# Small pads shift the split weights and the transposed activations to 96 bytes modulo 128

## The chip, the cores and the metric

The kernel runs on one core of a Trainium2 chip. The metric is the device time of one execution in microseconds: 2710.3 us before, the median of three runs between 2710.04 and 2711.56.

## The reference, cut to what matters

Two stacks of transformer blocks run one after the other on 256 tokens of width 1024, in float32. Nearly all of the arithmetic is large matrix products with weights that are used once.

```python
def conv_ffn(h, w_up, conv_w, conv_b, w_down):            # first stack, 2 blocks
    u = causal_dwconv(h @ w_up, conv_w, conv_b)
    g, val = jnp.split(u, 2, axis=-1)
    return (jax.nn.gelu(g) * val) @ w_down

def swiglu(x, w13, w2):                                   # second stack, twice in each of 4 blocks
    gate, up = jnp.split(x @ w13, 2, axis=-1)
    return (jax.nn.silu(gate) * up) @ w2
...
x = first_block(...)      # mixers: RG-LRU, gated linear attention
return second_block(...)  # mixers: sparse attention, forgetting attention, latent attention, sparse attention
```

## The kernel before

**Split products.** A float32 operand is split into a high part (`hi`, rounded to the type float32r) and a low part (`lo`, the rest). A product of two split operands is three TensorE matmuls: high by high, and the two mixed ones. `mm_b` (lines 432 to 434) keeps a block of transposed activations (128 by 128) in the array, as the stationary operand, and streams a weight piece of up to 512 columns past it, as the moving operand. `mm_a` (lines 439 to 441) does it the other way round: a 128 by 128 block of weights is stationary, and the 256 tokens of the transposed activations are moving. In a row of the trace the moving operand stands first: `u<-hThi,hi` streams `hThi` past stationary weights `hi`, `y<-hi,hT` streams weights `hi` past stationary activations `hT`.

**Weights.** One DMA on SyncE's queue brings a group of pieces, at most 1024 columns, into one of 4 buffers `raw`. ScalarE copies it into `hi` (line 369) and VectorE subtracts to give `lo` (line 370); both have 9 buffers in the kernel's long-lived pool `P`.

**Stages.** `Block1.run` opens a pool for each stage of the first stack; `Block2.run` keeps one pool `Q` for the second. In a feed-forward of the second stack the first two chunks of 256 hidden columns go through `mm_b` for each half of the tokens (the leads, stationary `hThi` and `hTlo`); the other nine go through `mm_a` in `ffn_both`; and the way down goes through `mm_b` with the hidden activations `hT` as stationary operand, 24 products after a chunk and 48 for each half of the tokens at the end. In the first stack the convolutional feed-forward does the same with `dhi` and `dlo`. Output projections use `oThi` and `oTlo` (second stack), `xchi` and `xclo` or `oT` (first stack) as stationary operand.

**What sets the order.** The order of the instructions is that of the Python code, with a scheduler that sees operations and buffers. A tile's address comes from its pool alone: tiles are laid one behind the other in the order in which they are first asked for, each rounded up to 32 bytes per partition. Every matmul operand here starts at a multiple of 128 bytes from its tile's start, except for pieces whose width isn't a multiple of 32 columns: the 272-column pieces of the forgetting attention (`mx1.v0`) and the 16-column blocks of `gla.z`.

Of the kernel before, what the change touches and what calls it, by code (L numbers as in the profile page):

```python
# [8 lines left out]
F32 = mybir.dt.float32  # L9
# [244 lines left out]
class _Cols:  # L254
    def __init__(self):
        self.at, self.parts, self.n = {}, [], 0
# [72 lines left out]
class Weights:  # L329
# [33 lines left out]
    def _load(self, g):  # L363
        nc = self.nc
        r, w = self._raw(g), self.groups[g][1]
        hi, lo = (self.pool.tile([128, w], F32R, name=f"{p}{g}", tag=p, bufs=self.nsp) for p in ("hi", "lo"))
        for a in range(0, w, self.step):
            b = min(a + self.step, w)
            nc.scalar.copy(out=hi[:, a:b], in_=r[:, a:b])  # L369
            nc.vector.tensor_tensor(out=lo[:, a:b], in0=r[:, a:b], in1=hi[:, a:b].bitcast(F32), op=OP.subtract)  # L370
        self.split[g] = (hi, lo)
# [5 lines left out]
class Kernel:  # L377
    def __init__(self, tc, a, out, plan, at, stages1, stages2):
        self.tc, self.nc, self.a, self.out, self.at = tc, tc.nc, a, out, at
        self.stages1, self.stages2 = stages1, stages2  # L380
        with ExitStack() as es:
            self.P = es.enter_context(tc.tile_pool(name="p", bufs=1))
            self.ps = es.enter_context(tc.tile_pool(name="ps", bufs=1, space=PSUM))
            self.ws = Weights(tc, self.P, a["w"], plan, 4, 9)
            self.idx = [0, 0]
            self.ident = self.P.tile([128, 128], F32, name="ident")
            make_identity(self.nc, self.ident)
            self.expo = self.P.tile([128, 4], F32, name="expo")
            self.nc.gpsimd.memset(self.expo, -0.5)
            self.first = {}  # L390

            self.hT = [self.P.tile([128, 8, 256], F32R, name=f"hT{p}") for p in ("hi", "lo")]
            self.x = [self.P.tile([128, D], F32, name=f"x{t}") for t in range(2)]
            for t in range(2):
                self.nc.sync.dma_start(out=self.x[t], in_=a["x"][t * 128:t * 128 + 128])
            if stages1:
                with tc.tile_pool(name="b1", bufs=1) as self.Q:
                    Block1(self).run()
            if stages2:
                self.ws.step = 512  # L400
                with tc.tile_pool(name="b2", bufs=1) as self.Q:
                    Block2(self).run()
            else:
                for t in range(2):
                    self.nc.sync.dma_start(out=out[0, t * 128:t * 128 + 128, :], in_=self.x[t])

    def small(self, name, w=1):
        return self.P.tile([128, w], F32, name=name, tag=f"sm_{name}_{w}", bufs=2)
# [59 lines left out]
class Block1:  # L468
# [534 lines left out]
    def run(self):  # L1003
        k = self.k
        self.ones = self.Q.tile([128, 128], F32, name="ones")
        self.V.memset(self.ones, 1.0)
        self.ada_init()
        end = x = None
        for st in k.stages1:
            i = {"rg": 0, "gla": 1}.get(st[0], st[-1])  # L1010
            w = int(st[0] == "cf")
            last = st == k.stages1[-1]
            if x is None and st[0] != "rg":
                x = self.h_tiles()
                mods = self.pre_mods(i, w)
                self.pre(0, mods, x)
                end = [1, mods, x]
            with k.tc.tile_pool(name=f"st_{st[0]}{i}", bufs=1) as self.R:
                stage = self.rg() if st[0] == "rg" else self.gla(x) if st[0] == "gla" else self.conv_ffn(i, x)
                if st[0] != "rg":  # L1020

                    next(stage)
                    self.pre(*end) if len(end) == 3 else self.turn(*end)
                self.due = self.left = DUE[i, w]
                self.share = 0.0
                y = next(stage)
                row = self.gate_row(i, w)
                h = None
                if not last:
                    mods = self.pre_mods(i + w, 1 - w)  # L1030
                    h = self.h_tiles()
                end = [0, y, row, mods if h else None, h]
                self.turn(*end)
                end[:2] = 1, next(stage)
                for _ in stage:
                    pass
                x = h
        if k.stages2:
            k.xt(0)
        self.turn(*end)  # L1040
        k.idx[1] = k.idx[0]


class Block2:
    def __init__(self, k):
        self.k, self.nc, self.a, self.P, self.Q = k, k.nc, k.a, k.P, k.Q
        self.V, self.ACT = k.nc.vector, k.nc.scalar
        self.gbt, self.shared, self.v, self.vt = {}, {}, [None, None], {}

    def gb(self, i):  # L1050
# [51 lines left out]

    def ht(self, key, c):

        if (key, c) not in self.hT:
            self.hT[key, c] = self.Q.tile([128, 2, 2, 256], F32R, name="hT", tag="kT", bufs=4)
        return self.hT[key, c]
# [93 lines left out]
    def attend(self, t, g, qh, kh, v, mask, scale, oT):  # L1201


        k, Q, V, ACT, nc = self.k, self.Q, self.V, self.ACT, self.nc
        nk = 128 * (t + 1)
        sm = k.small("sm", 4)

        sp = [k.bank("u", 4, (128, 2, 256)) for _ in range(2)]
        scores = [sp[e % 2][:, e // 2, :nk] for e in range(4)]
        for e in range(4):  # L1210
            nc.tensor.matmul(scores[e], qh(e), kh(e), start=True, stop=True)  # L1211
        probs = []
        for e in range(4):
            s = Q.tile([128, 256], F32, name="s", tag="s1k", bufs=5)[:, :nk]
            nb = k.small(f"nb{e}")
            V.tensor_tensor_reduce(out=s, in0=scores[e], in1=mask[:, :nk], scale=-scale, scalar=3.0e38,
                                   op0=OP.add, op1=OP.min, accum_out=nb)
            ACT.activation(out=s, in_=s, func=AF.Exp, scale=-1.0, bias=nb, accum_out=sm[:, e:e + 1])
            probs.append(s)
        rc = k.small("rc", 4)  # L1220
        V.reciprocal(out=rc, in_=sm)
        for e in range(4):
            V.tensor_scalar(out=probs[e], in0=probs[e], scalar1=rc[:, e:e + 1], scalar2=None, op0=OP.mult)
        pTs = []
        for e0 in (0, 2):
            pt = k.bank("u", 4, (128, 2, 2, 128))
            pT = Q.tile([128, 2, 2, 128], F32, name="pT", tag="pT", bufs=2)
            for e in range(2):
                for j in range(t + 1):
                    nc.tensor.transpose(pt[:, e, j, :], probs[e0 + e][:, j * 128:j * 128 + 128], k.ident)  # L1230
            (ACT.copy if e0 else V.tensor_copy)(out=pT[:, :, :t + 1, :], in_=pt[:, :, :t + 1, :])
            pTs.append(pT)

        op = k.bank("u", 4, (128, 2, 128))
        for e0 in (0, 2):
            for j in range(t + 1):
                for e in range(2):
                    nc.tensor.matmul(op[e * 64:e * 64 + 64, e0 // 2, :], v[j][:, e0 + e, :], pTs[e0 // 2][:, e, j, :],  # L1238
                                     start=j == 0, stop=j == t)
        if not oT:  # L1240
            oT += [Q.tile([128, 8, 128], F32R, name=f"oT{p}", tag=f"oT{p}{t}", bufs=1) for p in ("hi", "lo")]
        k.split(oT[0][:, g * 2:g * 2 + 2, :], oT[1][:, g * 2:g * 2 + 2, :], op)

# [312 lines left out]
```

## Time and profile before

| | |
|---|---|
| median of the runs | 2710.3 us |
| the profiled execution's own time | 2707.17 us |
| its span, first to last instruction | 2705.4 us |
| TensorE busy | 2643.8 us, 98% |
| VectorE busy | 1922.6 us, 71% |
| ScalarE busy | 1413.3 us, 52% |
| GpSimd busy | 76.6 us, 3% |
| weight loads into the array | 2335.4 us, 86%, beside the matmuls |
| read from HBM | 510.44 MB, 189 GB/s over the span |
| granted TensorE clock, mean | 0.996 of full speed |

A matmul's recorded duration runs from its start to its modelled end and overlaps the next ones, so durations of a line add up to more than the span. What a product costs in a stream is the step from its start to the start of the next. The stretches below run from the start of the first of N products to the start of the last, so that N-1 steps lie in them. The x in such a row counts what is busy in the stretch, and so also a product that began just before it.

### The profile page before, as it was taken

What the parts mean: (1) busy time and instruction counts of PE and PEld (TensorE: products, weight loads), DVE (VectorE), ACT (ScalarE), POOL (GpSimd) and SP (SyncE); (2) the same over time, 40 slices, a digit from 0 to 9 for tenths busy, and PEclk for the clock granted to TensorE, in tenths of its full rate; (3) what the DMA queues carried; (4) which work ended last, traced back from release to release, by engine and by line L of the source; (5) the groups of instructions that cost most, each with busy time, mean ns of one, the idle gap of its engine ahead of it and who ended that gap; (6) DMA issues with size and microseconds to landing.
All of it is one profiled execution on the core that took longest, in us unless ns stands there. A gap on an engine that the chain in (4) does not pass through costs nothing.

```text
span 2705.4 us, 44260 instructions
## 1 busy us (share of the span) xinstructions
PE 2643.8 (98%) x16680; PEld 2335.4 (86%) x16680; DVE 1922.6 (71%) x3876; ACT 1413.3 (52%) x2848; POOL 76.6 (3%) x115
## 2 busy tenths in 40 slices
PE   7899989999999999999999999999999999999998
PEld 5689977899899779989987899899889989977898
DVE  6889889877666886575666855756885575687755
ACT  4665664655444655444455544544754454456542
POOL 0000000000000000000000000000000000000000
PEclk9999999999999999999999999999999999999999
DMA  8868774665655547656654565664455565453652
GB/s 312 295 228 305 226 246 168 223 201 164 212 185 164 165 126 219 185 182 200 185 174 125 187 184 169 214 183 149 155 171 187 172 207 184 156 182 122 212 186 94
DMA packets 141081, 514.39 MB, mean 190 GB/s; under 512 B 16177, under 2 KB 16561, under 8 KB 139330
## 3 DMA queue, kind: packets, MB, share of 16 engines
q1 hardware_dynamic: 140866, 511.56, 58.9%
q8 instruction: 131, 2.15, 0.3%
q14 instruction: 84, 0.69, 0.1%
HBM read 510.44 MB, written 1.05 MB: 189 GB/s over the span
## 4 chain that ended last, share of the span: by engine, by line
PE 84%; issue 6%; DVE 5%; DMA 2%; ACT 2%; POOL 1%; DVEq 0%; POOLq 0%; SPq 0%; ACTq 0%
PE u L439 13%; PE u L440 13%; PE u L441 13%; PE y L432 11%; PE y L434 11%; PE y L433 11%; PE u L432 2%; PE u L433 2%; PE u L434 2%; DVE lo L370 2%; PE u L1211 1%; PE u L1238 1%; PE u L1230 1%; PE u L463 1%; DMA raw<-w 1%
## 5 line engine op out<-in xcount | busy, mean ns | idle before, releaser
L370 DVE TENSOR_TENSOR lo<-raw,hi 128x512 fp32r<-128x512 f32 (+4 forms) x1501 | 1080.7, 746 | 539.1 <-ACT hi L369 528.1
L369 ACT CAST hi<-raw 128x512 fp32r<-128x512 f32 (+4 forms) x1501 | 951.5, 666 | 772.0 <-issue 448.0
L439 PE MATMUL u<-hThi,hi 128*128 128x256 f32 x3016 | 857.4, 284 | 2.5 <-ACT hi L369 1.4
L440 PE MATMUL u<-hTlo,hi 128*128 128x256 f32 x3016 | 855.2, 284 | 0.0
L441 PE MATMUL u<-hThi,lo 128*128 128x256 f32 x3016 | 854.8, 284 | 0.2 <-DVE lo L370 0.2
L439 PEld LDWEIGHTS u<-hThi,hi 128*128 128x128 f32 x3016 | 578.8, 192 | 7.1 <-ACT hi L369 1.6
L440 PEld LDWEIGHTS u<-hTlo,hi 128*128 128x128 f32 x3016 | 579.1, 192 | 4.6 <-issue 1.0
L441 PEld LDWEIGHTS u<-hThi,lo 128*128 128x128 f32 x3016 | 578.8, 192 | 0.5 <-DVE lo L370 0.4
L432 PE MATMUL y<-hi,hT 128*128 128x512 f32 x704 | 279.1, 396 | 0.0
L433 PE MATMUL y<-lo,hT 128*128 128x512 f32 x704 | 278.6, 396 | 0.0
L434 PE MATMUL y<-hi,hT 128*128 128x512 f32 x704 | 278.4, 395 | 0.0
L432 PE MATMUL y<-hi,hThi 128*128 128x512 f32 (+6 forms) x504 | 189.3, 377 | 3.5 <-ACT hThi L444 3.3
L433 PE MATMUL y<-lo,hThi 128*128 128x512 f32 (+6 forms) x504 | 185.5, 369 | 0.1
L434 PE MATMUL y<-hi,hTlo 128*128 128x512 f32 (+6 forms) x504 | 184.1, 369 | 0.2 <-DVE hTlo L445 0.2
L434 PEld LDWEIGHTS y<-hi,hT 128*128 128x128 f32 x704 | 132.4, 188 | 31.9
L432 PEld LDWEIGHTS y<-hi,hT 128*128 128x128 f32 x704 | 132.6, 188 | 29.0
L433 PEld LDWEIGHTS y<-lo,hT 128*128 128x128 f32 x704 | 132.3, 188 | 28.8
L432 PE MATMUL u<-hi,hThi 128*128 128x512 f32 x320 | 127.0, 399 | 4.8 <-ACT hThi L444 4.8
L444 ACT CAST hT<-th 128x256 fp32r<-128x256 f32 x144 | 58.3, 405 | 130.2 <-DVE th L1100 130.2
L433 PE MATMUL u<-lo,hThi 128*128 128x512 f32 x320 | 125.8, 394 | 0.0
L434 PE MATMUL u<-hi,hTlo 128*128 128x512 f32 x320 | 124.2, 394 | 0.0
L432 PEld LDWEIGHTS y<-hi,hThi 128*128 128x128 f32 x504 | 94.9, 188 | 21.1 <-ACT hThi L444 5.2
(301 smaller groups left out, 3119.3 us busy)
## 6 DMA issues: line engine op xcount, KB each, us to landing
raw<-w SPq DMA_DIRECT2D x823, 512.0 KB, 3.7
adar<-ada SPq DMA_DIRECT2D x80, 512.0 KB, 4.8
gb<-lngb SPq DMA_DIRECT2D x12, 1024.0 KB, 5.2
adag<-ada SPq DMA_DIRECT2D x8, 512.0 KB, 5.4
adag<-adag SPq DMA_DIRECT2D x8, 512.0 KB, 5.7
raw<-w SPq DMA_DIRECT2D x8, 384.0 KB, 3.0
raw<-w SPq DMA_DIRECT2D x5, 480.0 KB, 3.5
raw<-w SPq DMA_DIRECT2D x4, 396.0 KB, 3.1
```

What stands on the lines that cost most here:

```text
L369: nc.scalar.copy(out=hi[:, a:b], in_=r[:, a:b])
L370: nc.vector.tensor_tensor(out=lo[:, a:b], in0=r[:, a:b], in1=hi[:, a:b].bitcast(F32), op=OP.subtract)
L432: mm(out, xhi, w[0], start=start, stop=False)
L433: mm(out, xhi, w[1], start=False, stop=False)
L434: mm(out, xlo, w[0], start=False, stop=stop)
L439: mm(out, whi, xhi, start=start, stop=False)
L440: mm(out, whi, xlo, start=False, stop=False)
L441: mm(out, wlo, xhi, start=False, stop=stop)
L444: self.nc.scalar.copy(out=hi, in_=src)
L463: self.nc.tensor.transpose(p[:, k * 128:k * 128 + 128], x[:, (h + k) * 128:(h + k + 1) * 128], self.ident)
L1211: nc.tensor.matmul(scores[e], qh(e), kh(e), start=True, stop=True)
L1230: nc.tensor.transpose(pt[:, e, j, :], probs[e0 + e][:, j * 128:j * 128 + 128], k.ident)
```

## The change

Four kinds of tile that nothing reads or writes are asked for at the right moments, so that the tiles behind them move up: 64 bytes per partition in front of `hi` and `lo`, 96 at the head of every stage's pool in the first stack, 96 in front of `hT`, 64 in front of `oThi` and `oTlo`.

```diff
     def _load(self, g):
         nc = self.nc
         r, w = self._raw(g), self.groups[g][1]
+        if not self.split:
+            self.pool.tile([128, 16], F32, name="padw")
         hi, lo = (self.pool.tile([128, w], F32R, name=f"{p}{g}", tag=p, bufs=self.nsp) for p in ("hi", "lo"))
...
+    def pad(self, pool, name, n):
+
+        pool.tile([128, n], F32, name=f"pad{name}")
...
             with k.tc.tile_pool(name=f"st_{st[0]}{i}", bufs=1) as self.R:
+                k.pad(self.R, st[0], 24)
...
     def ht(self, key, c):
 
+        if not self.hT:
+            self.k.pad(self.Q, "h", 24)
         if (key, c) not in self.hT:
...
         if not oT:
+            if not self.padded:
+                k.pad(Q, "o", 16)
+                self.padded = True
             oT += [Q.tile([128, 8, 128], F32R, name=f"oT{p}", tag=f"oT{p}{t}", bufs=1) for p in ("hi", "lo")]
```

The built programs of both kernels hold the same instructions in the same order on every engine, with the same waits, and differ in addresses alone. These are the addresses of the split operands, modulo 128 bytes:

| tile | role in a product | before | after |
|---|---|---|---|
| `hi`, `lo` | stationary in `mm_a`, moving in `mm_b` | 32 | 96 |
| `hThi`, `hTlo` | moving in `mm_a`, stationary in the leads and projections | 32 | 32 |
| `hT` | stationary on the way down, second stack | 64 | 96 |
| `dhi`, `dlo` | stationary on the way down, first stack | 64 | 96 |
| `xchi`, `xclo`, `oT` | stationary in output projections, first stack | 64 | 96 |
| `oThi`, `oTlo` | stationary in output projections, second stack | 0 | 96 |

`raw`, `x0` and `x1` stay at 32. The pads also move tiles that only VectorE, ScalarE and unsplit products use, for instance the working tiles `F`, `cv0` and `v0` from 64 to 96, `th` and `s` from 64 to 0, `adar` from 0 to 64.

## Rows read from the trace of the kernel before

**Rows 1.** The page: span, TensorE's busy time, granted clock by slice, chain by line.

```profile
span 2705.4 us, 44260 instructions
...
PE 2643.8 (98%) x16680; PEld 2335.4 (86%) x16680; DVE 1922.6 (71%) x3876; ACT 1413.3 (52%) x2848; POOL 76.6 (3%) x115
...
PEclk9999999999999999999999999999999999999999
...
PE u L439 13%; PE u L440 13%; PE u L441 13%; PE y L432 11%; PE y L434 11%; PE y L433 11%; PE u L432 2%; PE u L433 2%; PE u L434 2%; DVE lo L370 2%; PE u L1211 1%; PE u L1238 1%; PE u L1230 1%; PE u L463 1%; DMA raw<-w 1%
```

**Rows 2.** Groups by form: line, operands, shapes, count | busy us, mean ns | idle before.

```profile
L439 PE MATMUL u<-hThi,hi 128*128 128x256 f32 x3008 | 855.2, 284 | 2.5 <-ACT hi L369 1.4 <-DVE mn L910 1.1
...
L433 PE MATMUL y<-lo,hT 128*128 128x512 f32 x704 | 278.6, 396 | 0.0
...
L433 PE MATMUL y<-lo,hThi 128*128 128x512 f32 x352 | 139.5, 396 | 0.1
...
L433 PE MATMUL u<-lo,hThi 128*128 128x512 f32 x320 | 125.8, 394 | 0.0
...
L433 PE MATMUL y<-lo,dhi 128*128 128x512 f32 x176 | 69.8, 397 | 0.0
...
L433 PE MATMUL y<-lo,oThi 128*128 128x512 f32 x128 | 51.9, 405 | 0.0
...
L433 PE MATMUL y<-lo,oT 128*128 128x512 f32 x32 | 13.0, 406 | 0.0
...
L433 PE MATMUL y<-lo,xchi 128*128 128x512 f32 x32 | 12.9, 402 | 1.4 <-DVE lo L370 1.4
```

**Rows 3.** Six stretches: us, TensorE busy (x), granted clock, DMA share, GB/s.

```profile
144.22:154.89 10.67, 10.67 (x48) 1.00 0.72 245
841.75:863.90 22.15, 22.15 (x97) 1.00 0.36 106
1003.08:1010.13 7.05, 7.05 (x33) 1.00 0.58 181
...
1324.50:1358.93 34.43, 34.43 (x289) 1.00 0.59 171
1958.10:1960.66 2.56, 2.56 (x13) 1.00 0.00 0
318.38:327.94 9.56, 9.56 (x43) 1.00 0.59 196
```

**Rows 4.** TensorE in order of time, 272-column pieces: start us, us, line, operands.

```profile
1393.68 0.29 PE L432 MATMUL y<-hi,hThi 128*128 128x272 f32 x1
...
1394.06 0.29 PE L432 MATMUL y<-hi,hThi 128*128 128x272 f32 x1
...
1394.44 0.28 PE L432 MATMUL y<-hi,hThi 128*128 128x272 f32 x1
```

**Rows 5.** The same view, the 16-column blocks of gla.z.

```profile
369.75 0.28 PE L439 MATMUL u<-hThi,hi 128*16 128x256 f32 x1
...
370.10 0.28 PE L439 MATMUL u<-hThi,hi 128*16 128x256 f32 x1
...
370.45 0.28 PE L439 MATMUL u<-hThi,hi 128*16 128x256 f32 x1
```

**Rows 6.** Groups by form on VectorE and ScalarE: element work at different addresses.

```profile
L370 DVE TENSOR_TENSOR lo<-raw,hi 128x512 fp32r<-128x512 f32 x1291 | 849.8, 686 | 501.0 <-ACT hi L369 490.6
...
L938 DVE TENSOR_TENSOR F<-F,qT 128x512 f32<-128x512 f32 x8 | 5.5, 688 | 0.0
...
L369 ACT CAST hi<-raw 128x512 fp32r<-128x512 f32 x1291 | 752.2, 618 | 659.7 <-issue 448.0 <-PE y L434 94.9 <-DMA raw<-w 44.0
```

More of the change, by code (lines that the diff above doesn't have):

```diff
@@ L1047, in __init__ @@
         self.V, self.ACT = k.nc.vector, k.nc.scalar
+        self.padded = False
         self.gbt, self.shared, self.v, self.vt = {}, {}, [None, None], {}
```

## The prediction

> **What bounds the kernel now.** I read the page first. TensorE is busy for 98% of a span of 2705.4 us, the granted clock is full in every slice, and the chain that ended last is nearly all matmuls: `mm_a` has 39% of it, the lines of `mm_b` another 39% [rows 1]. VectorE (71%) and ScalarE (52%) mostly wait for each other's halves of a weight split. So time is the number of products times the step between two of them, and only a change of that step can pay.
>
> Then I looked for steps by operand address. The groups by form give the counts and who is stationary [rows 2]. Their mean durations run to a modelled end and hide most of the difference, so I took stretches in which one kind of product runs without a break and divided by the steps in them [rows 3]. All have a granted clock of 1.00, the 2.4 GHz level:
>
> - stationary `hThi` at 32, 512 columns: 48 products from 144.22, 10.67 us / 47 = 227.0 ns; 32 products from 1003.08 in the second stack, 7.05 / 31 = 227.4 ns
> - stationary `hT` at 64, 512 columns: 96 products from 841.75, 22.15 / 95 = 233.2 ns
> - stationary `dhi` at 64: 42 products from 318.38, 9.56 / 41 = 233.2 ns
> - stationary `oThi` at 0: 12 products from 1958.10, 2.56 / 11 = 232.7 ns
> - `mm_a`, stationary weights at 32, 256 columns: 288 products from 1324.50, 34.43 / 287 = 120.0 ns
>
> In all of them the moving operand lies at 32. So the step is not columns alone. From 256 to 512 columns with the stationary at 32 it grows by 227.4 - 120.0 = 107.4 ns; what is left of either, 12.6 ns, doesn't depend on the length. With the stationary at 64 or 0 that remainder is 18.4 ns. The address of the stationary block is the one thing that sorts the stretches: `hT`, `dhi` and `oThi` come from different stages, are written by different code, and agree to 0.5 ns, while the leads of the first and the second stack agree to 0.4 ns on the other level.
>
> **The change part by part.** No instruction, wait or queue position changes, so there is nothing to add but addresses.
>
> Way down and output projections, `mm_b` with the stationary going from 64 or 0 to 96. From the counts [rows 2], each for three lines: `hT` 704, `dhi` 176, `oThi` 128, `oT` 32, `xchi` 32, so 1072 x 3 = 3216 products of 512 columns. No stretch shows a full stationary block at 96. It lies 64 bytes from the good place, 32, and 32 bytes from each of the bad ones; and since 0 and 64, also 64 bytes apart, cost the same to 0.5 ns, I take it that the pattern repeats after 64 bytes and 96 costs what 32 costs. The gain is then 233.2 - 227.4 = 5.8 ns each: the second stack has most of these products, so its own stretches are the nearest rows. 3216 x 5.8 = 18.7 us. The ends are 2 ns, by which the recorded means of `y<-lo,hT` and `u<-lo,hThi` differ (396 and 394 ns), hence 6.4 us, and 233.2 - 227.0 = 6.2 ns, hence 19.9 us. All of it is on the path, since TensorE is what the end waits for.
>
> `mm_a`, stationary weights from 32 to 96, moving `hThi` still at 32: 3 x 3008 = 9024 products [rows 2]. By the same repeat after 64 bytes this costs nothing. The only rows with a stationary block at 96 are the 16-column blocks of `gla.z`, which lie 64 bytes apart: three products from 369.75 (at 96) take 0.35 us, three from 370.10 (at 32) take 0.35 us [rows 5]. That bounds the difference at 3 ns either way for an eighth of the columns, so it does not decide. Full blocks could move by as much as 0 and 64 differ from 32, 5.8 ns, either way: 52.3 us. I take 0 and keep both ends as rivals.
>
> Moving weights from 32 to 96 in every `mm_b`: the 272-column pieces lie at 32, 96, 32 in turn, past `hThi` at 32. Three products from 1393.68 (at 96) take 0.38 us, three from 1394.06 (at 32) take 0.38 us [rows 4]. I take 0; the resolution leaves 3 ns for each.
>
> Element work on moved tiles: the subtraction of 512 columns with all operands at 32 takes 686 ns, a multiplication of as many with all operands at 64 takes 688 ns [rows 6]. Two nanoseconds on 1291 splits are 2.6 us of an engine that idles a quarter of the span, so they cost nothing; were that cover gone, they would cost 2.6 us. TensorE running 0.7% faster asks the same of the splits: in the densest stretch, `mm_a` from 1324.50, the DMA share is 0.59 [rows 3], and ScalarE's copy idled 660 us in all, of which 44 us waited for a landing [rows 6]. I see nothing that comes late next.
>
> **Sum.** 18.7 us off. Against the profiled execution's own 2707.2 us (span 2705.4 and 1.8 around it) that gives 2688.5. The median of the runs lies 3.1 us above that execution, so the forecast is 2710.3 - 18.7 = 2691.6, say 2692.
>
> **The rivals.**
>
> *96 is a bad place for a stationary block.* The rows have one good residue, 32, and it might be the only one. Then `hT`, `dhi` and the rest go from one bad place to another, and `mm_a` leaves the good one: 9024 x 5.8 = 52 us more, 2763 us. A penalty of 18.7 us / 9024 = 2.1 ns on `mm_a` already eats the whole gain, since it has nearly three times as many products. A variant of it: 32 is good because the moving operand lies there too. Then the way down (96 and 96) gains its 19 us, `mm_a` (96 past 32) loses 52, and the total is still about 33 us slower or more. For it: nothing here shows 96 at work on a full block. Against it: 0 and 64 agree, and three products with the moving operand 64 bytes from the stationary one run as fast as with both in one place [rows 4].
>
> *96 is better than 32.* 12.6 ns of a step of `mm_a` do not come from columns, so there is something to win; if 96 took off another 5.8 ns there, as 32 does against 64, `mm_a` would bring 52 us on top: 2710.3 - 18.7 - 52.3 = 2639. No row speaks for it but the size of the remainder; the `gla.z` blocks at 96 show no gain.
>
> *Addresses don't matter.* The 5.8 ns could belong to the role, not to the address: `hThi` is always the input of a stage, the others are always its output. Then nothing moves: 2710. Against it stands that three tiles of two stacks, written by different code and read among different neighbours, share the slow level, at 0 and at 64, while the one tile at 32 has the fast level in both stacks. The Trainium skill speaks for this rival: "TensorE: Matmul & The Clock Gate", in "Step-by-step: what each phase is for", says that TensorE has two independent read ports into SBUF, one for the streaming operand and one for weight loads, so that loading the next block takes nothing from the running product. By that rule all 512-column steps would be equal and the sum would be 0; the stretches at 227.4 and 233.2 ns [rows 3] disagree with it, unless their difference has another cause than an address.
>
> **How the numbers follow.** The forecast, 96 like 32: 0.50; its own range, by the ends above, is 2690 to 2704. 96 better: 0.16, 2639. Nothing moves: 0.14, 2710 give or take 2. 96 bad: 0.20, about 2743 to 2763. The range takes in the first three and leaves the last out, since it alone has the 2 in 10 that may be left: 2639 to 2712. About 0.2%, 5.4 us, is what a measurement of this kernel can tell from no change; faster is the first two, 0.66; same 0.14; slower 0.20.
>
> **What would show it right or wrong.** In the profile after: the step of `y<-hi,hT`, over 96 products at a feed-forward's end, falls from 233.2 to about 227 ns, and so do the steps with `dhi` and `oThi`; the step of 288 products of `mm_a` stays at 120.0 ns; leads stay at 227. If `mm_a` steps at 122 ns or more, the first rival holds; at 118 or less, the second; if the way down stays at 233 and `mm_a` at 120, the third. TensorE's idle time before `mm_a` should stay at a few microseconds; were it to grow, the splits have become late and my cover for them was wrong.

## The result, and the profile after

The median goes from 2710.17 us (2707.53 to 2711.56) to 2663.8 us (2662.09 to 2668.03), four runs each: a ratio of 0.9832 with an interval of 0.9815 to 0.9849, so 46.4 us less. The forecast was 18.7 us less, 2692, with a range from 2639 to 2712. Direction and range held; the size was 2.5 times the forecast, and nearly all of it came from the product for which I had put down nothing.

In the numbering of the kernel after, `mm_b` is lines 438 to 440, `mm_a` 445 to 447, the copy into `hi` 371 and the subtraction that gives `lo` 372. First the page: span and busy time of the engines, the granted clock by slice, and the groups that answer to [rows 1, 2].

```profile
span 2662.2 us, 44260 instructions
...
PE 2598.1 (98%) x16680; PEld 2287.7 (86%) x16680; DVE 1919.3 (72%) x3876; ACT 1413.6 (53%) x2848; POOL 75.3 (3%) x115
...
PEclk9999999999999999999999999999999999999999
...
L445 PE MATMUL u<-hThi,hi 128*128 128x256 f32 x3016 | 840.1, 279 | 2.4 <-ACT hi L371 1.4
...
L445 PEld LDWEIGHTS u<-hThi,hi 128*128 128x128 f32 x3016 | 567.7, 188 | 7.1 <-DVE mn L916 1.6
```

The same instructions at the same clock: TensorE's busy time fell by 2643.8 - 2598.1 = 45.7 us, VectorE's by 3.3 us and ScalarE's not at all. One product of `mm_a` lasts 279 ns where it lasted 284.

Then the stretches, read as in [rows 3]: us, TensorE busy (x), granted clock, DMA share, GB/s. In order: 96 products of the way down with `hT`; 32 of the leads in the second stack; 96 of `mm_a` behind the first way down of a feed-forward (48 products); 96 behind the second (24 products); 288 of `mm_a`; 12 with `oThi`; 42 with `dhi` in the first stack.

```profile
835.33:857.40 22.07, 22.07 (x98) 1.00 0.36 113
996.68:1003.78 7.10, 7.10 (x33) 1.00 0.56 193
1042.54:1053.73 11.19, 11.19 (x97) 1.00 0.63 190
1059.41:1070.19 10.78, 10.78 (x96) 1.00 0.64 195
1125.28:1157.82 32.54, 32.54 (x289) 1.00 0.62 193
...
1939.67:1942.21 2.54, 2.54 (x13) 1.00 0.20 77
...
316.36:326.41 10.05, 9.80 (x43) 1.00 0.66 210
```

Divided by the steps in them:

| stretch | before | after |
|---|---|---|
| `mm_a`, 288 products | 120.0 ns | 32.54 / 287 = 113.4 ns |
| `mm_a`, 96 products behind the second way down | 120.0 | 10.78 / 95 = 113.5 |
| `mm_a`, 96 products behind the first way down | 120.0 | 11.19 / 95 = 117.8 |
| way down, `hT` | 233.2 | 22.07 / 95 = 232.3 |
| leads, `hThi` | 227.4 | 7.10 / 31 = 229.0 |
| `oThi` | 232.7 | 2.54 / 11 = 230.9 |
| first stack, `dhi` | 233.2 | 10.05 / 41 = 245.1, with 0.25 us idle in it |

So where did the 43.2 us between the two profiled executions come from (2707.2 and 2664.0)? I added the steps from the start of each product to the start of the next, by kind, over the whole of both traces: `mm_a` went from 1088.8 to 1042.2 us, -46.6; the way down with `hT` from 493.0 to 491.4, -1.6; the leads from 488.0 to 490.1, +2.1. The products with `dhi`, `xchi` and `oT` of the first stack cost 5.2 us more (127.4 to 130.4, 26.5 to 28.4, 25.8 to 26.1), everything else 1.3 us less. Together that is -42.3 us, and 0.8 us lies ahead of the first product.

The first stack kept almost nothing. Its `mm_a` won 6.6 us, but its leads took 1.3 us more, and of the 5.2 us more for `dhi`, `xchi` and `oT` the larger part is waiting for producers. Here is who TensorE waited for, in the profile after and behind it in the profile before: us in total, times, longest.

```profile
PE y L438 <- ACT dhi L450: 2.5, 4, 1.2
...
PE y L440 <- DVE dlo L451: 1.4, 5, 0.3
...
PE y L438 <- ACT hi L371: 1.2, 1, 1.2
```

```profile
PE y L432 <- ACT dhi L444: 1.3, 1, 1.3
```

Before, it waited once for the copy into `dhi`, for 1.3 us, and not at all for `dlo`; after, nine times for 3.9 us, and once more for 1.2 us ahead of a product with `xchi`. The start of the same product tells it too: the 4001st matmul, shortly behind the first stack, starts at 706.5 us after and 708.1 us before, 1.6 us earlier. The other 41.6 us came behind it.

### The profile page after: what moved, and what is told of

It reads as the page before. It is cut to its first block, busy times and chain, and to the rows that moved or that the text cites. A ratio compares the mean times of both kernels' runs of the same rounds, so it can differ in the third digit from the quotient of the medians.

```text
span 2662.2 us, 44260 instructions
## 1 busy us (share of the span) xinstructions
PE 2598.1 (98%) x16680; PEld 2287.7 (86%) x16680; DVE 1919.3 (72%) x3876; ACT 1413.6 (53%) x2848; POOL 75.3 (3%) x115
## 4 chain that ended last, share of the span: by engine, by line
PE 78%; issue 8%; DVE 7%; DMA 3%; ACT 2%; POOL 1%; DVEq 0%; SPq 0%; POOLq 0%; ACTq 0%
PE u L445 11%; PE u L446 11%; PE u L447 11%; PE y L438 10%; PE y L440 10%; PE y L439 10%; PE u L438 3%; PE u L439 3%; PE u L440 3%; DVE lo L372 2%; DMA raw<-w 2%; DMA adar<-ada 1%; PE u L1221 1%; PE u L469 1%; PE u L1248 1%
## 5 line engine op out<-in xcount | busy, mean ns | idle before, releaser
L445 PE MATMUL u<-hThi,hi 128*128 128x256 f32 x3016 | 840.1, 279 | 2.4 <-ACT hi L371 1.4
L447 PE MATMUL u<-hThi,lo 128*128 128x256 f32 x3016 | 837.0, 278 | 0.6 <-DVE lo L372 0.6
L446 PE MATMUL u<-hTlo,hi 128*128 128x256 f32 x3016 | 837.5, 278 | 0.0
L445 PEld LDWEIGHTS u<-hThi,hi 128*128 128x128 f32 x3016 | 567.7, 188 | 7.1 <-DVE mn L916 1.6
L446 PEld LDWEIGHTS u<-hTlo,hi 128*128 128x128 f32 x3016 | 567.6, 188 | 4.7 <-issue 1.0
L447 PEld LDWEIGHTS u<-hThi,lo 128*128 128x128 f32 x3016 | 569.1, 189 | 1.2 <-DVE lo L372 1.0
```

What stands on the lines that cost most here:

```text
L445: mm(out, whi, xhi, start=start, stop=False)
L446: mm(out, whi, xlo, start=False, stop=False)
L447: mm(out, wlo, xhi, start=False, stop=stop)
```

## The experiments

All kernels here compute the whole result. In the expectations, theory A (later A256) is that the step depends on the *distance*, the address of the stationary block minus that of the moving block, and no longer on either alone; theory B is my prediction's reading, that the stationary block's own place decides. Places are given modulo 128 bytes, as in the section on the change. "Distance" is always the difference modulo 256 bytes. These are the distances of the main kinds of product, from the addresses in the built programs:

| kernel | `mm_a` | leads | `hT` | `dhi`, `xchi`, `oT` | `oThi` |
|---|---|---|---|---|---|
| before | 0 | 0 | 32 | 32 | 96 |
| after | 64 | 192 | 128 | 128 | 0 |
| weights alone | 64 | 192 | 96 | 96 | 160 |
| activations alone | 0 | 0 | 64 | 64 | 192 |
| both at 96 | 0 | 0 | 64 | 32 | 224 |
| swapped | 64 | 192 | 96 | 128 | 192 |
| every distance its best | 64 | 192 | 0 | 0 | 0 |

**Halves of the change.** The first run moves the weights alone, the second the activations alone.

```diff
-                k.pad(self.R, st[0], 24)
+                k.pad(self.R, st[0], 16)
-            self.k.pad(self.Q, "h", 24)
+            self.k.pad(self.Q, "h", 16)
-                k.pad(Q, "o", 16)
+                pass
```

> Only the split weights go to 96 modulo 128; hT, dhi, xchi and oT stay at 64, oThi at 0, hThi at 32. If the gain of the change is the weights' alone, mm_a steps at 113 to 114 ns as after the change, and the time is 2710 - 9024 x 5.6 ns = 2660 plus what the 512-column products lose: about 2664. Theory A (what counts is the distance between stationary and moving block): the way down, stationary 64 past moving 96, is 32 apart as before, so it stays at 233. Theory B (what counts is the stationary block's own address): the same, 233, since it stays at 64. If instead the activations' move is needed, the time stays above 2690.

Measured: 2672.16 us, ratio 0.9854 (0.9839 to 0.9868). Rows: 96 products of the way down, 288 of `mm_a`.

```profile
836.83:859.07 22.24, 22.24 (x98) 1.00 0.33 119
1127.44:1159.99 32.55, 32.55 (x288) 1.00 0.63 194
```

```diff
-            self.pool.tile([128, 16], F32, name="padw")
+            pass
-                k.pad(self.R, st[0], 24)
+                k.pad(self.R, st[0], 8)
-            self.k.pad(self.Q, "h", 24)
+            self.k.pad(self.Q, "h", 8)
```

> Only the transposed activations hT, dhi, xchi, oT and oThi go to 96; the split weights stay at 32 with hThi at 32. mm_a stays at 120 ns. Theory A: the way down, stationary 96 past moving 32, is 64 apart like mm_a after the change, so it should gain as mm_a did, to 226 ns or less: 3216 x 6 = 19 us, about 2691. Theory B, an own address of 96 is fast: the same gain. If 96 gives the way down 232 whatever the moving block's place, the time is 2707 or so, no change.

Measured: 2711.3 us, ratio 0.9999 (0.9989 to 1.0009). The same two stretches:

```profile
844.60:866.77 22.17, 22.17 (x97) 1.00 0.34 109
1137.76:1172.18 34.42, 34.42 (x288) 1.00 0.56 184
```

The weights carry the change: with them alone at 96, `mm_a` steps in 32.55 / 287 = 113.4 ns. Without them, activations at 96 bring nothing: 22.17 / 95 = 233.4 ns, where both theories had forecast 226 or less. So 64, the distance at which `mm_a` is fast, is a slow one for 512 columns: the same rule does not hold for both lengths. Beside the moved weights the activations' move does pay: with the weights alone the time is 6 to 8 us above the kernel after, more than the expectation's 2664, and the way down then steps in 22.24 / 95 = 234.1 ns, at distance 96, against 232.3.

**Own place or distance.** The third kernel puts `hThi` and the weights both at 96, the fourth puts `hThi` at 96 and the weights at 32; the other pads keep the rest where it is needed.

```diff
+            self.pad(self.P, "t", 16)
             self.hT = [self.P.tile(
...
-            self.pool.tile([128, 16], F32, name="padw")
+            pass
```

> hThi and the split weights both at 96 (and raw, x at 96); hT at 32, dhi, xchi and oT at 0, oThi at 64. Theory A: mm_a's blocks are 0 apart as before the change, 120 ns; the leads 0 apart, 227 ns. Theory B: stationary weights at 96 are fast, mm_a at 113 to 114 ns. The way down shows stationary blocks at 32, 0 and 64 past moving 96.

Measured, one run: 2710.34 us. Rows: way down, leads, `mm_a`.

```profile
842.69:864.86 22.17, 22.17 (x97) 1.00 0.33 114
1004.06:1011.09 7.03, 7.03 (x32) 1.00 0.55 192
1135.93:1170.34 34.41, 34.41 (x288) 1.00 0.59 184
```

> The places of after are swapped: hThi at 96, the split weights at 32; hT at 0, dhi, xchi and oT at 32, oThi at 96. Theory A (distance): 64 apart again, mm_a at 113 to 114 ns. Theory B (own address of the stationary block): weights at 32 as before, 120 ns. A third, C, that the moving block's own address counts: 113 or less if 96 is a better place for the moving block, 120 if it doesn't matter.

Measured, one run: 2665.63 us; its diff is the added line above, with the weights' pad kept and two other pads changed. The same three stretches:

```profile
831.89:854.13 22.24, 22.24 (x97) 1.00 0.38 110
993.37:1000.46 7.09, 7.09 (x32) 1.00 0.60 187
1122.44:1154.99 32.55, 32.55 (x288) 1.00 0.62 192
```

These two settle it. With both operands at 96 the leads step in 7.03 / 31 = 226.8 ns and `mm_a` in 34.41 / 287 = 119.9, as with both at 32 before; the weights lie there at the same place as after the change, even modulo 256 (224), so their own place is not what makes `mm_a` fast. With weights at 32 (modulo 256 they are at 32 there and at 160 before) past `hThi` at 96, `mm_a` takes 113.4 ns, as after. `hThi` lies at 96 in both kernels, with 119.9 and with 113.4 ns, so the moving block's own place doesn't decide either. No residue is good or bad by itself; the distance sorts the steps.

**Every distance its best.** By that theory the way down should have distance 0 (its best) and `mm_a` 64. So this kernel (e9 in the expectations) keeps the weights where the change puts them and moves the activations of `mm_b` on by 128 bytes.

```diff
-                k.pad(self.R, st[0], 24)
+                k.pad(self.R, st[0], 56)
-            self.k.pad(self.Q, "h", 24)
+            self.k.pad(self.Q, "h", 56)
-                k.pad(Q, "o", 16)
+                k.pad(Q, "o", 48)
```

> Distances are now taken modulo 256 (stationary minus moving). The weights stay where the change puts them (mm_a 64 apart, 113 to 114 ns), and hT, dhi, xchi, oT and oThi go to the very residue of the weights, 0 apart modulo 256; after the change they are 128 apart (oThi 0). Theory A256: the way down steps at 228 ns like the leads before the change, 3216 products less 384 at oThi gain 4 ns each, 11 us on the time after the change: about 2652. Rival R (the way down's 232 to 234 ns belong to its role, not to any address): no gain, 2664.

Measured: 2678.59 us, ratio 0.9871 (0.9854 to 0.9888), slower than the kernel after. Rows: way down, 96 and 288 products of `mm_a`.

```profile
836.82:858.35 21.53, 21.53 (x97) 1.00 0.38 110
1060.18:1071.37 11.19, 11.19 (x97) 1.00 0.64 190
1127.16:1160.97 33.81, 33.81 (x289) 1.00 0.64 188
```

Half of it came as expected: the way down steps in 21.53 / 95 = 226.6 ns, so 128 is not the period of the pattern (after has distance 128 there, and 232.3 ns). The other half is a surprise: `mm_a` steps in 117.8 ns though its operands lie at the same places, modulo 256, as in the kernel after, which has 113.4.

**The other distances.** Four kernels like the last one, with another pad in front of the weights (the pools behind move along, so the way down stays at distance 0): 32, 96, 192 and 128 bytes between weights and `hThi`.

```diff
-            self.pool.tile([128, 16], F32, name="padw")
+            self.pool.tile([128, 8], F32, name="padw")
```

> Weights 32 bytes behind hThi modulo 256, the way down at distance 0. Theory A256: the way down at 228 ns, the leads at 224 apart, near 233 ns as oThi showed there; mm_a at a distance not yet seen: between 113 and 120 if the step rises and falls smoothly with distance. Rival R: way down at 232 to 234.

> Weights 96 bytes behind hThi modulo 256, the way down at distance 0. Theory A256: the way down at 228 ns, the leads (160 apart) near 233 ns. mm_a is new: 113 to 120; if 512-column products tell of it (234 at 96, the highest), 120 or more.

> Weights again at 96 modulo 128 as in the change, but in the other half of 256 bytes: 192 behind hThi. If 128 bytes is the period (the change's own premise), mm_a steps at 113 to 114 as after it and the time is the same. Theory A256: a distance of its own, so another step than 113.5, and the leads at 64 apart, 233.4 ns.

> mm_a at the one distance not yet seen among the multiples of 32 bytes up to 128: weights 128 behind hThi modulo 256, the way down at distance 0, the leads at 128. By the distances seen (0: 120.0, 32: 118.3, 64: 113.3 or 117.8, 96: 118.7, 192: 117.8) I expect 117 to 120 and leads at 232; if 128 has a faster step of its own, 113 or less.

Measured, one run each: 2697.13, 2699.51, 2690.58 and 2705.2 us. The stretch of 288 products of `mm_a` in the four, in that order:

```profile
1134.76:1168.72 33.96, 33.96 (x288) 1.00 0.62 187
```

```profile
1135.85:1169.91 34.06, 34.06 (x289) 1.00 0.64 187
```

```profile
1134.34:1168.14 33.80, 33.80 (x288) 1.00 0.63 188
```

```profile
1136.97:1171.40 34.43, 34.43 (x288) 1.00 0.59 184
```

That is 118.3, 118.7, 117.8 and 120.0 ns. The way down, at distance 0 in all four but each time at another place, steps in 227 ns throughout (21.55 to 21.58 us for 95 steps). All the stretches of all runs together give this picture (means of the steps between products of one kind, those over 6% above the median, which hold waits, left out):

| distance, modulo 256 | 0 | 32 | 64 | 96 | 128 | 160 | 192 | 224 |
|---|---|---|---|---|---|---|---|---|
| 512 columns (`mm_b`), ns | 228.0 | 233.1 | 233.4 | 233.9 | 232.3 | 233.4 | 229.5 | 233.1 |
| 256 columns (`mm_a`), ns | 120.0 | 118.3 | 113.3 or 117.8 | 118.7 | 120.0 | not run | 117.8, a few 113.3 | not run |

At 512 columns, 0 and 128 differ, and so do 64 and 192: the pattern doesn't repeat after 128 bytes. It does after 256: distances that agree modulo 256 but not modulo 512 have the same step (233.0 and 233.1 ns at 32, 232.3 and 232.3 at 128). The distances of `mm_a` all lay in one half of 512 bytes, so for 256 columns that period is not shown. Tiles of different stages at one distance mostly agree to 1.5 ns. The exception is `oThi`, whose products come in runs of 18 at most and mostly of 6 or fewer: at distance 0 it has 230.1 ns where `hT` has 226.7, both in the kernel with every distance at its best. Why is not shown.

**Two steps at one distance.** At distance 64 a run of `mm_a` keeps either 113.3 or 117.8 ns from its first few products to its last. After has both, as the third and the fourth of its stretches above show: of the 48 runs behind a way down in the second stack, the first of each of the 8 feed-forwards has 117.8 and the other 40 have 113.3, at the same distances. The kernel with every distance at its best has 117.8 in all 48. Is it the last product ahead of the run that chooses? Two kernels mix both distances in the way down, by a wider tile for `hT` (and, in the first, the pads in front of `hT` and `oThi` of the kernel with the best distances): the first has distance 0 for its high part and 128 for its low part, which comes last of the three products; the second has it the other way round.

```diff
-            self.hT[key, c] = self.Q.tile([128, 2, 2, 256], F32R, name="hT", tag="kT", bufs=4)
+            self.hT[key, c] = self.Q.tile([128, 2, 2, 288], F32R, name="hT", tag="kT", bufs=4)[:, :, :, :256]
```

> At 64 apart mm_a has two steps that hold through a whole run of 96 or 288 products, 113.3 and 117.8 ns: after the change it enters the first behind a way down at distance 128, in e9 the second behind a way down at distance 0. Here everything is as after the change, but the high part of hT lies at distance 0 and its low part, the stationary block of the last product ahead of mm_a, at 128. Theory L (the last product ahead decides the step that locks): mm_a at 113.3 as after the change, the way down at about (227 + 227 + 232) / 3 = 229 ns, 2112 x 3.5 = 7 us better than after the change: about 2657. Rival M (most of the products ahead decide, or the residue of the tile): 117.8, about 2682.

Measured: 2687.38 us, ratio 0.9912 (0.9896 to 0.9927). Way down and `mm_a`:

```profile
839.03:860.98 21.95, 21.95 (x97) 1.00 0.37 111
1130.42:1164.23 33.81, 33.81 (x289) 1.00 0.63 187
```

> The mirror: the high part of hT stays at distance 128 as after the change, only the low part, ahead of mm_a, goes to distance 0. Theory L: mm_a locks at 117.8, about 8 FFNs x 768 products x 4.5 ns = 28 us slower than after the change, less 2 us on the way down: about 2690. Rival M: 113.3 as after the change, 2662.

Measured, one run: 2688.3 us. The same two stretches:

```profile
834.61:856.78 22.17, 22.17 (x97) 1.00 0.35 110
1126.55:1160.35 33.80, 33.80 (x288) 1.00 0.61 187
```

Both have 117.8 ns, so the distance of the last product ahead doesn't choose; that theory falls. The rival, that most of the products ahead decide, falls with the second kernel, for which it had 113.3. The way down adds something: taken apart by line, the first kernel's three steps are 226.7, 232.6 and 234.1 ns. Only the product whose own block and whose successor's block both lie at distance 0 is fast, so one foreign distance among three spoils two steps. In the second kernel no two blocks in a row lie at distance 0, and none of the three is fast. In the mean it is 21.95 / 95 = 231.1 ns for the first and 22.17 / 95 = 233.4 for the second.

To know that the kernel after itself was stable, it ran once more beside them.

> The changed kernel itself, on the same chip as the others of this call: 2664 within 5 us; mm_a at 113.3 behind every way down.

Measured: 2666.45 us, ratio 0.9835 (0.982 to 0.9851), again with 113.3 ns in 40 of the 48 runs behind a way down. The expectation said all of them; the first of each feed-forward has 117.8, as in the first profile.

**A kick at the entry.** If the moment at which a run is entered chooses, and not the addresses, then a small shift in time should flip it. These kernels have the addresses of the one with the best distances, and split the second product of each run of `mm_a` in the second stack's feed-forwards in two (56 runs, 48 of them behind a way down): 64 and 192 columns, 128 and 128, 192 and 64.

```diff
+                            if c <= NCH - FW + 1 and not (j or s or kk):
+                                mm = self.nc.tensor.matmul
+                                mm(u[:, s, :], w[0][:, sl], x[0][:, kk, :], start=True, stop=False)
+                                mm(u[:, s, :64], w[0][:, sl], x[1][:, kk, :64], start=False, stop=False)
+                                mm(u[:, s, 64:], w[0][:, sl], x[1][:, kk, 64:], start=False, stop=False)
+                                mm(u[:, s, :], w[1][:, sl], x[0][:, kk, :], start=False, stop=False)
+                                continue
```

> The same with 64 and 192 columns, another disturbance of the entry. By the moment of entry it may lock at 113.3 (2651) where 128 does not, or the other way round; by addresses 117.8 (2679).

> All addresses as in e9; the second product of every run of mm_a behind a way down streams its 256 columns as 128 and 128. If the moment of entry chooses the step, some or all runs lock at 113.3 ns: 8 x 768 x 4.5 = 28 us off e9's 2679, 2651. If addresses choose: 117.8 and 2679 or a little more (56 extra products of some 10 ns, under 1 us).

> The same with 192 and 64 columns. The three together say whether any disturbance of the entry flips the step: by the moment of entry at least one of them steps at 113.3, by addresses none does.

Measured: 2658.91 us (0.9804, 0.9787 to 0.982), 2659.01 us (0.9804, 0.9789 to 0.9819), and 2687.99 us in one run. The entry with 64 columns in order of time (start us, us, line, operands), and then the 93 products of `mm_a` that follow the split, in the first kernel and in the third:

```profile
1040.24 0.28 PE L1159 MATMUL u<-hThi,hi 128*128 128x256 f32 x1
1040.36 0.20 PE L1160 MATMUL u<-hTlo,hi 128*128 128x64 f32 x1
1040.39 0.33 PE L1161 MATMUL u<-hTlo,hi 128*128 128x192 f32 x1
1040.56 0.30 PE L1162 MATMUL u<-hThi,lo 128*128 128x256 f32 x1
1040.70 0.28 PE L445 MATMUL u<-hThi,hi 128*128 128x256 f32 x1
```

```profile
1040.70:1051.14 10.44, 10.44 (x94) 1.00 0.65 197
```

```profile
1047.23:1058.06 10.83, 10.83 (x93) 1.00 0.63 193
```

10.44 / 92 = 113.5 ns against 10.83 / 92 = 117.7, at the same addresses. So addresses allow the short step, and what happens at the entry decides whether it is taken: two of three kicks flip all 48 runs behind a way down, the third flips none.

It is not the length of the delay, though. From the first product of the run to the first one behind the split the kernel with 64 columns takes 1040.70 - 1040.24 = 0.46 us; these are the same two products with 128 and with 192 columns first:

```profile
1041.88 0.28 PE L1159 MATMUL u<-hThi,hi 128*128 128x256 f32 x1
...
1042.34 0.28 PE L445 MATMUL u<-hThi,hi 128*128 128x256 f32 x1
```

```profile
1046.76 0.28 PE L1159 MATMUL u<-hThi,hi 128*128 128x256 f32 x1
...
1047.23 0.28 PE L445 MATMUL u<-hThi,hi 128*128 128x256 f32 x1
```

That is 0.46 and 0.47 us, so all three push what follows back by about as much, and they differ in the starts inside the entry. A plain shift in time without a split was not run.

The two kernels with a flip are faster than the kernel before by 52 us. They lie 5 to 8 us below the kernel after, but their intervals (to 0.982) and its own (from 0.9815) still touch.

At distances 0 and 64 the recorded weight loads go with the step. These are the page's groups of loads of `mm_a` before, then with the best distances and no kick, then with the kick of 64, then of 192:

```profile
L439 PEld LDWEIGHTS u<-hThi,hi 128*128 128x128 f32 x3016 | 578.8, 192 | 7.1 <-ACT hi L369 1.6
```

```profile
L447 PEld LDWEIGHTS u<-hThi,lo 128*128 128x128 f32 x3016 | 577.5, 192 | 0.6 <-DVE lo L372 0.4
L445 PEld LDWEIGHTS u<-hThi,hi 128*128 128x128 f32 x3016 | 567.1, 188 | 7.1 <-DVE mn L916 1.6
```

```profile
L445 PEld LDWEIGHTS u<-hThi,hi 128*128 128x128 f32 x2960 | 556.8, 188 | 5.5 <-ACT hi L371 2.4
L447 PEld LDWEIGHTS u<-hThi,lo 128*128 128x128 f32 x2960 | 558.5, 189 | 1.8 <-DVE lo L372 1.6
```

```profile
L445 PEld LDWEIGHTS u<-hThi,hi 128*128 128x128 f32 x2960 | 565.5, 191 | 4.2 <-ACT hi L371 1.6
L447 PEld LDWEIGHTS u<-hThi,lo 128*128 128x128 f32 x2960 | 557.8, 188 | 0.5 <-DVE lo L372 0.4
```

In a run at 117.8 ns one load of three is recorded at 192 ns and two at 188; in one at 113.3 all are at 188; before, at 120.0, all are at 192. The kick of 192 moved the long load from the third product to the first, and did not remove it. At other distances the mark fails. These are the longest loads at distance 192, where a run has 117.8 ns, and at distance 128, where it has 120.0:

```profile
L447 PEld LDWEIGHTS u<-hThi,lo 128*128 128x128 f32 x3016 | 567.4, 188 | 0.6 <-DVE lo L372 0.4
```

```profile
L445 PEld LDWEIGHTS u<-hThi,hi 128*128 128x128 f32 x3016 | 571.9, 190 | 6.6 <-ACT hi L371 1.6
```

So a long load is not what makes a step long; it comes with it at some distances.

## Why the prediction was wrong

- *The bound.* TensorE stayed the bound, no other engine became one, and the element work on moved tiles cost nothing: VectorE's busy time went from 1922.6 to 1919.3 us. That held. One reading on the way was wrong and changed nothing: [rows 6] put 448 of the 660 us that ScalarE's copy idled down to issue and none to VectorE, so VectorE waits for ScalarE and not the other way round.
- *The step that failed: "The address of the stationary block is the one thing that sorts the stretches", and from it "the pattern repeats after 64 bytes and 96 costs what 32 costs".* In every stretch of [rows 3] the moving operand lay at one place, so own address and distance could not be told apart there, and I took the one that I could see. The leads were fast because their distance was 0, not because 32 is a good place. The runs with both operands at 96 (226.8 ns for the leads, 119.9 for `mm_a`) and with the two swapped (113.4 ns for `mm_a`) show it.
- *Way down, 3216 x 5.8 = 18.7 us.* Mis-sized: its step fell by 0.9 ns, from 233.2 to 232.3, and the sum over `hT` by 1.6 us. The change puts it at distance 128. At distance 0, which 128 bytes more of padding give, the forecast 227 ns did come (226.6).
- *`mm_a`, 9024 products at no change.* Mis-sized the other way: the mean step without waits fell from 119.8 to 114.2 ns, 5.6 ns, which is 50.5 us for 9024 and 46.6 us in the sum of its steps, waits included. I had kept 5.8 ns either way as its ends, so the second rival's price was nearly right for this term, and its sign in "118 or less". That was luck, and so is it that the time lies inside the range, whose lower end came from this rival. Its reason, that 96 is better than 32, is wrong: with both operands at 96, `mm_a` steps as before. Nor were the 12.6 ns a fixed remainder that an address could take a part of: the same working from the fastest steps, 226.6 and 113.3 ns, leaves nothing.
- *The rows at 96 that I leaned on.* The 272-column and the 16-column pieces [rows 4, 5] could not show a difference under 3 ns, and were three products long; the steps at a run's entry are not yet those that it settles on (before the change the first nine of a run of `mm_a` behind a way down average 118 ns, and then it holds 120.0). They should have had less weight against the rivals. The section on the kernel left out the 264-column pieces of the sparse attention, which start 32 and 64 bytes on too; their steps, 122 ns in the median at each of three places, would not have told more.
- *The variant of the first rival*, that 32 is good because the moving operand lies there too, was the right kind of mechanism. I gave its terms the wrong signs, since I took equal addresses modulo 128 as best for every product. They are for 512 columns, and only modulo 256; for 256 columns distances 0 and 128, at 120.0 ns, are the worst measured.
- *The leads stay at 227.* They went to 229.0, since the weights moved away from them: distance 192. It cost 2.1 us.
- *"I see nothing that comes late next".* Right for the second stack. In the first `mm_a` won 6.6 us, and the products with `dhi`, `xchi` and `oT` took back 5.2 us, much of it in waits for the copy and the subtraction.
- *"Addresses don't matter".* The Trainium skill, "TensorE: Matmul & The Clock Gate", "Step-by-step: what each phase is for", says that TensorE has two independent read ports, so that a weight load takes nothing from the running product. Here the step moved by 6 ns with the addresses of the two operands alone, so what the rival drew from that rule, equal steps at all addresses, does not hold for these float32r products; which part of the chip the two meet in, no run here shows.

What stays open: what at the entry of a run picks 113.3 or 117.8 ns. That splitting a product there can flip it at unchanged addresses is shown; that it is a matter of the moment is not, nor which moment would be the good one. `mm_a` at distances 160 and 224, or at two distances 256 bytes apart, was not run.

## What to carry to other kernels

Where each product loads a new block, measure the step between starts for each kind of product against the distance between its two operands, modulo 256 bytes (shown as the period at 512 columns; at 256 columns it only fits), not against either address, and vary both operands before calling one of them the cause. The best distance for one shape (0 at 512 columns) was the worst for another (256 columns), so weigh each kind by its count. And a step of a few nanoseconds can depend on how a run is entered: a layout that is best for each kind alone came out 12 to 15 us slower than the kernel after (2678.6 against 2666.5 and 2663.8).

## What the runs showed that I had not expected

- Steps of float32r products depend on the distance of stationary and moving operand (modulo 256 bytes, as far as shown): 226.6 to 234 ns at 512 columns, 113.3 to 120.0 ns at 256.
- At one distance a run can keep two different steps, 113.3 or 117.8 ns, over 288 products; splitting one product at the entry of 56 runs changed 2678.59 us to 2658.91.
- At distances 0 and 64 the recorded length of a weight load goes with it: 192 ns for each at 120.0 ns, for one in three at 117.8, 188 ns for each at 113.3. At 128 and 192 it doesn't: 188 to 190 ns at 120.0, 187 to 188 at 117.8.
- A kind of step can be spoiled by its neighbours: one distance of 128 among three products left one fast step of three (226.7, 232.6, 234.1 ns).
